# Attention scores in an encoder: stacked high and low parts of queries and keys on 128 partitions, in place of 32-bit products on 64

## The chip, the core and the metric

The kernel runs on one core of a Trainium2 chip. The metric is the device time of one execution in microseconds, median of three runs. TensorE is called PE here, with its weight loads as PEld; VectorE is DVE, ScalarE is ACT, GpSimd is POOL, and SP issues the transfers from HBM.

## The reference, cut to what matters

Two layers, each of them feed-forward, mixer, feed-forward on an input of 256 rows and 1024 columns in float32. The change lies in the mixer's attention.

```python
def hybrid_mixer(x, w_in, sc_conv_w, attn_sink, cc_conv_w, cc_conv_b, cc_ln_g, cc_ln_b, w_out):
    ...
    z = x @ w_in
    sc_b, sc_c, sc_h, q, k, v, cc_a, cc_gate = jnp.split(z, IN_OFFSETS, axis=-1)
    y_sc = sc_b * depthwise_conv(sc_c * sc_h, sc_conv_w)
    q = rope(q.reshape(b, s, N_Q_HEADS, HEAD_DIM), positions)      # 8 heads of 64
    k = rope(k.reshape(b, s, N_KV_HEADS, HEAD_DIM), positions)     # 2 heads of 64
    v = v.reshape(b, s, N_KV_HEADS, HEAD_DIM)
    y_att = banded_window_attention(q, k, v, attn_sink)
    u = cc_a * jax.nn.sigmoid(cc_gate)
    u = depthwise_conv(u, cc_conv_w) + cc_conv_b                   # 31 taps, 256 channels
    y_cc = jax.nn.silu(layer_norm(u, cc_ln_g, cc_ln_b))
    return jnp.concatenate([y_sc, y_att, y_cc], axis=-1) @ w_out

def reference(x, ...):
    for l in range(DEPTH):
        x = layer_norm(ALPHA * x + 0.5 * swiglu(x, ffn1_w_gu[l], ffn1_w_down[l]), ...)
        x = layer_norm(ALPHA * x + hybrid_mixer(x, ...), ...)
        x = layer_norm(ALPHA * x + 0.5 * swiglu(x, ffn2_w_gu[l], ffn2_w_down[l]), ...)
    return x
```

## The kernel before

**Products.** Nearly every float32 product is made as three products of high and low parts (`mm3`: high by high, high by low, low by high), with the parts in the type `F32R`. `split` makes the parts: ACT casts the high part (L96), and DVE subtracts it from the source to get the low part (L97). Weights come in blocks of 128 by 2048 through `fetch` (SP) and `emit_block` (cast and subtract). In each mixer nine of its blocks are listed in `POOL_BLOCKS`; the low part of these is made on POOL in four pieces. A block's buffers come free when its last product has read them, and the cast of a later block waits for that.

**The scores** are the exception: `scores(t, i)` (L542 to L551) takes the turned queries `qT` and keys `kT` in plain float32, 64 partitions (one head's channels) at a time, one product for each head, and adds the window mask by a bf16 product with the identity. A call is a unit of four heads; there are four units in a layer, two for each half of the rows. `q_turned` and `k_turned` transpose on PE into a PSUM bank and copy the bank to SBUF on ACT.

**The mixer** runs in this order: the gate's and queries' projections, keys and values (`kv`), the convolution's three projections (`proj_c` into `psc`, `psh`, `psb`), and in between the four attention units: scores `S_`, softmax, transposes of the probabilities `T_`, product with the values `V_`. The 31 taps of the conformer convolution for two channel groups (62 instructions in a layer, L531 and L533, accumulated in two PSUM banks) run on DVE; `fill(n)` puts n of them into the program at places where DVE was thought to have room, and the rest follows ahead of `T_(3)`. When the last tap is done, PE transposes the convolution's result (`cc_norm`), and the last parts of the output projection (`w_out`, `w_out2`) and the norm at the mixer's boundary follow. `T_(3)`, `w_out2(0, 2)`, `cc_norm`, `V_(3)`, `w_out2(1, 2)`, `cc_out`, `w_out2(1, 0)` and `w_out2(0, 1)` stand in this order in the program.

```python
        w_out2(0, 0)
        fill(62)
        T_(3)
        w_out2(0, 2)
        uns = cc_norm()
        V_(3)
        accs.append([bank() for _ in range(2)])
        new_norm = Norm()
        w_out2(1, 2)
        cc_out(uns)
        w_out2(1, 0)
        w_out2(0, 1)
```

**Order and buffers.** A scheduler places the instructions of each engine in an order of its own, by the program's order and its idea of when each is ready; on the chip each engine runs its list in that order and waits at an instruction whose inputs or buffers are not ready. The pool `mm` has four PSUM banks; while the taps run, two of them hold the convolution, and two are left for everything that is called `tmp`. The pool `gbp` has one buffer, tag `gb`, for the gains and biases of a boundary's norm; it is not in use during the attention.

Of the kernel before, what the change touches and what calls it, by code (L numbers as in the profile page):

```python
# [8 lines left out]
F32 = mybir.dt.float32  # L9
F32R = mybir.dt.float32r  # L10
BF16 = mybir.dt.bfloat16
AF = mybir.ActivationFunctionType
ALU = mybir.AluOpType
# [3 lines left out]
P = 128  # L17
D = 1024
S = 256
# [5 lines left out]
HD = 64  # L25
# [21 lines left out]
def encoder(ctx: ExitStack, tc: tile.TileContext, head_in, xt_in, x_in, w_in, gb_in, small_in, rope_in, out):  # L47
    nc = tc.nc
# [7 lines left out]
    gbp = pool("gbp", 1)  # L56
    st = pool("st", 4)
    mx = pool("mx", 1)
# [29 lines left out]
    def tmp_bank():  # L88
        return phase["pool"].tile([P, 512], F32, tag="mm", name="tmp")
# [113 lines left out]
    def transpose(ps, srcs):  # L203
        for i, a in enumerate(srcs):
            nc.tensor.transpose(ps[:, i * P:(i + 1) * P], a, ident)  # L205
# [252 lines left out]
    def mixer(l, norm):  # L458
# [11 lines left out]
        nc.gpsimd.memset(upad, 0.0)  # L470
        ppad = mx.tile([P, 2, S + 2], F32, tag="ppad", name="ppad")
        nc.gpsimd.memset(ppad, 0.0)
        kT = mx.tile([P, S], F32, tag="kT", name="kT")
        half = HD // 2
        chan = lambda a: a.rearrange("p (c n) -> p c n", c=2)

# [22 lines left out]
        def q_turned(r):  # L499
            pq = tmp_bank()  # L500
            transpose(pq, [r[:, c * P:(c + 1) * P] for c in range(4)])
            q = mx.tile([P, 4, P], F32, tag="qT", bufs=2, name="qT")
            nc.scalar.copy(q.rearrange("p c n -> p (c n)"), pq)
            return q

        def k_turned(t, r):
            pk = tmp_bank()
            transpose(pk, [r[:, 0:P]])
            nc.scalar.copy(kT[:, t * P:(t + 1) * P], pk[:, 0:P])

        def kv(t, w):
            ps = tmp_bank()
# [29 lines left out]
        def scores(t, i):  # L542
            mo = 1 - t
            scs = [chan(bank()) for _ in range(2)]
            for c in range(2):
                for j in range(2):
                    hp = slice(j * HD, (j + 1) * HD)
                    nc.tensor.matmul(scs[j][:, c, :], qT[t][hp, 2 * i + c, :], kT[hp, :], start=True, stop=False)
                for j in range(2):
                    nc.tensor.matmul(scs[j][:, c, mo * P:(mo + 1) * P], ident_b, mask[:, t, :], start=False, stop=True)  # L550
            return scs  # L551
# [81 lines left out]
        qT, vn, rk = [], [], []  # L633
        ga, q = bank(), bank()
# [7 lines left out]
        ga, q = bank(), bank()  # L642
# [12 lines left out]
        v, rk0 = kv(0, wkv)  # L655
        vn.append(v)
        fill(6)
        v, rk1 = kv(1, wkv)
# [3 lines left out]
        fill(6)  # L662
        proj_c(psc, wc, 0)
        qT.append(q_turned(r1))
        k_turned(0, rk0)
        k_turned(1, rk1)
        fill(5)
        proj_c(psc, wc, 1)
        scc = big()
# [6 lines left out]
        def S_(u):  # L676
            return scores(u // 2, u % 2)
# [41 lines left out]
        scs = S_(3)  # L719
# [144 lines left out]
```

## Time and profile before

| what | value |
|---|---|
| median of 3 runs | 935.26 us (935.13 to 937.06) |
| the profiled execution: its time, its span | 937.28 us, 935.5 us |
| PE busy | 921.8 us (99%) |
| DVE busy | 645.4 us (69%) |
| ACT busy | 458.1 us (49%) |
| POOL busy | 116.9 us (12%) |
| mean granted clock of PE | 0.995 |

The profiled execution took 2.0 us more than the median. The shares are averages over the whole span. The mixers, which the change touches, are about 216 to 285 us and 678 to 745 us after the span's start.

### The profile page before, as it was taken

How to read it: one execution, taken by the hardware profiler on the slowest of the kernel's cores; microseconds unless marked ns; L12 is line 12 of the kernel's file. 1: busy time of each engine (PE TensorE's matmuls, PEld its weight loads, DVE VectorE, ACT ScalarE, POOL GpSimd, SP SyncE). 2: the span in 40 equal slices, each digit the busy share in tenths (PEclk: the TensorE clock that was granted, in tenths of full speed). 3: DMA queues.
4: the chain of work that ended last, by engine and by line, in shares of the span. 5: the costliest groups of instructions: out<-in, count | busy, mean ns of one | idle time of the engine just before them, and what ended most of it. 6: DMA issues, size and time to landing. Idle time of an engine off the chain costs nothing.

```text
span 935.5 us, 12113 instructions
## 1 busy us (share of the span) xinstructions
PE 921.8 (99%) x4900; PEld 778.7 (83%) x4900; DVE 645.4 (69%) x811; ACT 458.1 (49%) x593; POOL 116.9 (12%) x108
## 2 busy tenths in 40 slices
PE   9999999999999999999999999999999999999996
PEld 6888888888777888888888888888887788888885
DVE  6966556789967756665777665667799766666545
ACT  6644554345744554445345445454456455444530
POOL 0010000009282000000000000000274800000000
PEclk9999999999999999999999999999999999999998
DMA  9976465546234655454456545544551366555301
GB/s 345 376 249 257 175 222 183 180 140 224 88 102 181 257 211 195 178 187 177 179 187 230 213 180 198 202 171 150 216 190 57 139 247 224 189 180 188 128 1 45
DMA packets 25976, 174.01 MB, mean 186 GB/s; under 512 B 2880, under 2 KB 3136, under 8 KB 5696
## 3 DMA queue, kind: packets, MB, share of 16 engines
q1 hardware_dynamic: 25920, 173.24, 51.5%
q8 instruction: 38, 0.62, 0.3%
q14 instruction: 18, 0.15, 0.0%
HBM read 172.18 MB, written 1.05 MB: 185 GB/s over the span
## 4 chain that ended last, share of the span: by engine, by line
PE 88%; DVE 7%; ACT 1%; POOL 1%; issue 1%; DMA 1%; SPq 0%; DVEq 0%; ACTq 0%
PE wide L170 28%; PE wide L174 15%; PE bank L153 9%; PE bank L154 9%; PE bank L155 9%; PE bank L181 4%; PE bank L185 4%; PE bank L182 4%; DVE tmp L533 3%; PE bank L195 1%; PE tmp L205 1%; POOL lo L97 1%; PE tmp L596 1%; PE bank L205 1%; DVE x L234 1%
## 5 line engine op out<-in xcount | busy, mean ns | idle before, releaser
L97 DVE TENSOR_TENSOR lo<-raw,hi 128x2048 fp32r<-128x2048 f32 (+2 forms) x175 | 317.1, 1825 | 211.1 <-ACT hi L96 210.8
L96 ACT CAST hi<-raw 128x2048 fp32r<-128x2048 f32 (+2 forms) x247 | 306.4, 1270 | 241.2 <-PE wide L170 154.2
L170 PE MATMUL wide<-xT,hi 128*128 128x512 f32 x1152 | 274.1, 390 | 0.0
L170 PEld LDWEIGHTS wide<-xT,hi 128*128 128x128 f32 x1152 | 213.9, 188 | 43.0
L174 PEld LDWEIGHTS wide<-xT,lo 128*128 128x128 f32 x1152 | 147.7, 191 | 5.6
L174 PE MATMUL wide<-xT,lo 128*128 128x256 f32 x1152 | 149.4, 283 | 0.0
L153 PE MATMUL bank<-hi,hh 128*128 128x512 f32 x352 | 137.7, 391 | 0.0
L154 PE MATMUL bank<-lo,hh 128*128 128x512 f32 x352 | 137.4, 390 | 0.0
L155 PE MATMUL bank<-hi,hl 128*128 128x512 f32 x352 | 137.0, 389 | 0.0
L97 POOL TENSOR_TENSOR lo<-raw,hi 128x512 fp32r<-128x512 f32 x72 | 95.9, 1366 | 67.2 <-ACT hi L96 66.8
L228 POOL TENSOR_TENSOR rstd<-ve,mhalf 128x1 f32<-128x1 f32 x12 | 11.5, 961 | 672.0 <-DVE ve L227 672.0
L155 PEld LDWEIGHTS bank<-hi,hl 128*128 128x128 f32 x352 | 66.1, 188 | 14.0
L153 PEld LDWEIGHTS bank<-hi,hh 128*128 128x128 f32 x352 | 66.2, 188 | 12.7
L154 PEld LDWEIGHTS bank<-lo,hh 128*128 128x128 f32 x352 | 66.2, 188 | 12.3
L96 ACT CAST hh<-big 128x512 fp32r<-128x512 f32 x36 | 22.3, 620 | 110.2 <-DVE big L358 110.2
L181 PE MATMUL bank<-hi,xT 128*128 128x512 f32 x160 | 64.7, 404 | 0.0
L182 PE MATMUL bank<-lo,xT 128*128 128x512 f32 x160 | 62.6, 391 | 0.0
L366 DVE TENSOR_TENSOR big<-wide,big 128x512 f32<-128x512 f32 x72 | 49.2, 684 | 6.9 <-ACT big L365 6.9
L533 DVE SCALAR_TENSOR_TENSOR tmp<-upad,wc,tmp 128x256 f32<-128x256 f32 x116 | 49.7, 477 | 0.2
L365 ACT COPY big<-wide 128x512 f32<-128x512 f32 x72 | 42.3, 587 | 11.9 <-PE wide L174 11.6
L185 PE MATMUL bank<-hi,xT 128*128 128x512 f32 x160 | 43.2, 392 | 0.0
L97 DVE TENSOR_TENSOR hl<-big,hh 128x512 fp32r<-128x512 f32 x36 | 24.9, 693 | 24.0 <-ACT hh L96 24.0
(130 smaller groups left out, 890.5 us busy)
## 6 DMA issues: line engine op xcount, KB each, us to landing
raw<-in_w SPq DMA_DIRECT2D x152, 1024.0 KB, 4.8
gb<-in_gb SPq DMA_DIRECT2D x6, 1024.0 KB, 4.9
raw<-in_w SPq DMA_DIRECT2D x4, 512.0 KB, 7.5
head<-in_head SPq DMA_DIRECT2D x4, 384.0 KB, 4.6
raw<-in_w SPq DMA_DIRECT2D x4, 256.0 KB, 7.7
x<-in_x SPq DMA_DIRECT2D x2, 512.0 KB, 5.7
out<-x SPq DMA_DIRECT2D x4, 256.0 KB, 2.1
xraw<-in_xt SPq DMA_DIRECT2D x2, 256.0 KB, 8.0
```

The source lines that it names most:

```text
L96: nc.scalar.copy(hi, src)
L97: (eng or nc.vector).tensor_tensor(lo, src, hi.bitcast(F32), ALU.subtract)
L153: nc.tensor.matmul(ps, ah, bh, start=first, stop=False)
L154: nc.tensor.matmul(ps, ah, bl, start=False, stop=False)
L155: nc.tensor.matmul(ps, al, bh, start=False, stop=last)
L170: nc.tensor.matmul(ps[:, c], w[0][:, k, cs], xT[:, :, k], start=k == 0, stop=False)
L174: nc.tensor.matmul(ps[:, c, 0], w[1][:, k, cs], xT_h[:, k], start=False, stop=k == KC - 1)
L181: nc.tensor.matmul(ps, xT_h[:, kk, t, :], w[0][:, k, :], start=kk == 0, stop=False)
L182: nc.tensor.matmul(ps, xT_h[:, kk, t, :], w[1][:, k, :], start=False, stop=False)
L185: nc.tensor.matmul(ps, xT_l[:, kk, t, :], w[0][:, k, :], start=False, stop=kk == KC - 1)
L366: nc.vector.tensor_tensor(av, ps[:, :, 0], av, ALU.add)
L533: nc.vector.scalar_tensor_tensor(dst, upad[:, c, k:k + S], wc2[:, c, k:k + 1], part, op0=ALU.mult, op1=ALU.add)
```

## The change

Queries and keys are each split into a high and a low part, and the parts of one head are laid on both halves of the 128 partitions. For head j of the two key heads, `qT[:, j]` has the high part on the partitions of the head and the low part on the other 64; `kT[:, j, 0]` has the key's high part on both halves and `kT[:, j, 1]` its low part on both. Two products over 128 partitions then give the sum of all four products of parts. `keep`, in the slot of `gb`, holds the keys and the first half's queries; the second half's queries stay in a tile of their own with one buffer. Both key transposes now go into one PSUM bank, and one call of `k_turned` makes all of `kT`. For a layer this takes away two ACT copies of 128x512 and two of 128x128; it adds four ACT casts of 64x512 and four DVE subtracts of the same size for the queries (two halves of the rows, two heads), and four ACT casts and four DVE subtracts of 64x256 for the keys (two heads, two halves of the partitions).

```diff
-        kT = mx.tile([P, S], F32, tag="kT", name="kT")
+
+        keep = gbp.tile([P, 2, D], F32, tag="gb", name="keep").bitcast(F32R)
+        kT = keep[:, 0].rearrange("p (j x n) -> p j x n", j=2, x=2)
...
             transpose(pq, [r[:, c * P:(c + 1) * P] for c in range(4)])
-            q = mx.tile([P, 4, P], F32, tag="qT", bufs=2, name="qT")
-            nc.scalar.copy(q.rearrange("p c n -> p (c n)"), pq)
+            if qT:
+                q = mx.tile([P, 2, 4, P], F32R, tag="qT", name="qT")
+            else:
+                q = keep[:, 1].rearrange("p (j c n) -> p j c n", j=2, c=4)
+            for j in range(2):
+                own, other = (slice(i * HD, (i + 1) * HD) for i in (j, 1 - j))
+                flat = q[:, j].rearrange("p c n -> p (c n)")
+                nc.scalar.copy(flat[own], pq[own])
+                nc.vector.tensor_tensor(flat[other], pq[own], flat[own].bitcast(F32), ALU.subtract)
             return q
 
-        def k_turned(t, r):
+        def k_turned(rs):
+
             pk = tmp_bank()
-            transpose(pk, [r[:, 0:P]])
-            nc.scalar.copy(kT[:, t * P:(t + 1) * P], pk[:, 0:P])
+            transpose(pk, [r[:, 0:P] for r in rs])
+            for j in range(2):
+                own = slice(j * HD, (j + 1) * HD)
+                for half in range(2):
+                    to = slice(half * HD, (half + 1) * HD)
+                    nc.scalar.copy(kT[to, j, 0], pk[own, 0:S])
+                for half in range(2):
+                    to = slice(half * HD, (half + 1) * HD)
+                    nc.vector.tensor_tensor(kT[to, j, 1], pk[own, 0:S], kT[own, j, 0].bitcast(F32), ALU.subtract)
...
             for c in range(2):
                 for j in range(2):
-                    hp = slice(j * HD, (j + 1) * HD)
-                    nc.tensor.matmul(scs[j][:, c, :], qT[t][hp, 2 * i + c, :], kT[hp, :], start=True, stop=False)
+                    for part in range(2):
+                        nc.tensor.matmul(scs[j][:, c, :], qT[t][:, j, 2 * i + c, :], kT[:, j, part], start=part == 0, stop=False)
...
         qT.append(q_turned(r1))
-        k_turned(0, rk0)
-        k_turned(1, rk1)
+        k_turned((rk0, rk1))
```

The scheduler's order moves too. The first place is PE's list around the key transposes of layer 0. Before, they (`tmp_1936`, `tmp_1939`) stand inside `proj_c(psc)`'s second half (`tmp_1886`), each in a bank of its own:

```order
L205 MATMUL tmp_1936<-ident_85,big_1829 128x128 [waits Activation_49]
L153 MATMUL tmp_1886<-xT_96,hi38_1729 128x256
L154 MATMUL tmp_1886<-xT_96,hi38_1729 128x256
L155 MATMUL tmp_1886<-xT_96,lo38_1730 128x256
L153 MATMUL tmp_1886<-xT_96,hi38_1729 128x256
L205 MATMUL tmp_1939<-ident_85,big_1880 128x128 [waits DVE_49,Activation_49]
```

Now both go into one bank (`tmp_1941`, the one that the second queries' transposes had before), behind the whole of that projection (now `tmp_1888`), and the first scores (`bank_1983`) stand inside the next one (`tmp_2020`, which is `psh`):

```order
L155 MATMUL tmp_1888<-xT_96,lo38_1730 128x256
L205 MATMUL tmp_1941<-ident_85,big_1831 128x128 [waits DVE_49,PE_49]
L205 MATMUL tmp_1941<-ident_85,big_1882 128x128
L153 MATMUL tmp_2020<-xT_96,hi39_1760 128x256 [waits Activation_49]
L154 MATMUL tmp_2020<-xT_96,hi39_1760 128x256
L155 MATMUL tmp_2020<-xT_96,lo39_1761 128x256
L153 MATMUL tmp_2020<-xT_96,hi39_1760 128x256
L154 MATMUL tmp_2020<-xT_96,hi39_1760 128x256
L565 MATMUL bank_1983<-keep_1616 128x256 [waits Activation_49]
```

The first of the key transposes now waits for DVE, where the second queries' last subtract reads that bank.

The second place is DVE's list behind the rotation of the last keys. Before, 15 taps stand there in a row (L533), and the first unit's maximum (L558) follows. Now the subtracts of the second queries (L512) and of the keys (L526) stand between the taps (L550 by the new numbers); these are the rows from the second of the two query subtracts on:

```order
L512 TENSOR_TENSOR qT_1936<-tmp_1931,qT_1936 64x512 [waits Activation_49]
L550 SCALAR_TENSOR_TENSOR tmp_1771<-upad_1612,wc2_1608,tmp_1771 128x256 [waits DVE_49]
L550 SCALAR_TENSOR_TENSOR tmp_1772<-upad_1612,wc2_1608,tmp_1772 128x256 [waits DVE_49]
L550 SCALAR_TENSOR_TENSOR tmp_1771<-upad_1612,wc2_1608,tmp_1771 128x256 [waits DVE_49]
L550 SCALAR_TENSOR_TENSOR tmp_1772<-upad_1612,wc2_1608,tmp_1772 128x256 [waits DVE_49]
L526 TENSOR_TENSOR keep_1616<-tmp_1941,keep_1616 64x256 [waits PE_49,Activation_49]
L526 TENSOR_TENSOR keep_1616<-tmp_1941,keep_1616 64x256
L550 SCALAR_TENSOR_TENSOR tmp_1771<-upad_1612,wc2_1608,tmp_1771 128x256 [waits DVE_49]
L550 SCALAR_TENSOR_TENSOR tmp_1772<-upad_1612,wc2_1608,tmp_1772 128x256 [waits DVE_49]
L575 TENSOR_REDUCE mxs_1998<-bank_1983 128x2 [waits PE_49]
L526 TENSOR_TENSOR keep_1616<-tmp_1941,keep_1616 64x256 [waits Activation_49]
```

The taps that were there move to the end: 16 of them now stand in a row as the last of the layer, where 9 did.

The third place is PE's list at the end of the mixer. Before, the transposes of the convolution's result (`tmp_2385`, `tmp_2386`) follow on the output projection's block `hi41` for the first half of the rows (`bank_2316`), with the products of the last unit's values between them (L596), and `hi41` for the second half (`bank_2418`) comes next:

```order
L155 MATMUL bank_2316<-hi41_1835,yhl_1622 128x512
L205 MATMUL tmp_2385<-ident_85,big_1768 128x128 [waits DVE_49,PE_49]
L205 MATMUL tmp_2386<-ident_85,big_1768 128x128 [waits PE_49]
L596 MATMUL tmp_2411<-big_2364,vn_1827 64x256 [waits Activation_49]
L205 MATMUL tmp_2385<-ident_85,big_1768 128x128 [waits DVE_49]
L205 MATMUL tmp_2386<-ident_85,big_1768 128x128
L596 MATMUL tmp_2411<-big_2364,vn_1878 64x256
L596 MATMUL tmp_2411<-big_2371,vn_1827 64x256 [waits DVE_49]
L596 MATMUL tmp_2411<-big_2371,vn_1878 64x256
L153 MATMUL bank_2418<-hi41_1835,yhh_1621 128x512 [waits PE_49]
```

Now twelve products of the block `hi43` (into `bank_2341` and `bank_2342`, the last of them in the first row here) stand ahead of these transposes (now `tmp_2411`, `tmp_2412`):

```order
L155 MATMUL bank_2342<-hi43_2045,yhl_1620 128x512
L205 MATMUL tmp_2411<-ident_85,big_1770 128x128 [waits DVE_49,PE_49]
L205 MATMUL tmp_2412<-ident_85,big_1770 128x128
L613 MATMUL tmp_2437<-big_2390,vn_1829 64x256 [waits Activation_49]
L205 MATMUL tmp_2411<-ident_85,big_1770 128x128 [waits DVE_49]
L205 MATMUL tmp_2412<-ident_85,big_1770 128x128
L613 MATMUL tmp_2437<-big_2390,vn_1880 64x256
L613 MATMUL tmp_2437<-big_2397,vn_1829 64x256 [waits DVE_49]
L613 MATMUL tmp_2437<-big_2397,vn_1880 64x256
L153 MATMUL bank_2444<-hi41_1837,yhh_1621 128x512 [waits PE_49]
```

Before, those twelve stood behind `hi42`'s products for the second half. So the last read of `hi41` has moved behind them, and with it the cast of the block that takes its buffer (`hi46`, of the feed-forward behind the mixer).

## Rows read from the trace of the kernel before

**Rows 1.** The page, part 1: busy time of each engine.

```profile
PE 921.8 (99%) x4900; PEld 778.7 (83%) x4900; DVE 645.4 (69%) x811; ACT 458.1 (49%) x593; POOL 116.9 (12%) x108
```

**Rows 2.** Chain that ended last, layer 0's mixer: start, us, what.

```profile
222.79 5.88 DVE tmp L533 x15
...
265.99 0.63 ACT hi L96
...
278.25 0.97 POOL rstd L228
279.25 2.45 DVE x L234 x2
...
284.25 1.19 PE bank L185 x4
```

**Rows 3.** Stretches: length, busy of PE, PEld, DVE, ACT, POOL, then granted clock.

```profile
216.00:260.00 44.00, 43.24 (x306) 35.29 (x305) 42.39 (x106) 28.66 (x83) 26.11 (x22) 0.96 0.35 123
678.00:722.00 44.00, 43.24 (x314) 35.13 (x314) 43.27 (x107) 28.94 (x83) 26.53 (x22) 1.00 0.36 128
240.00:244.00 4.00, 4.00 (x24) 3.90 (x23) 3.57 (x8) 4.00 (x14) 3.90 (x4) 0.60 0.00 0
```

**Rows 4.** Timeline of DVE: start, us, engine, line, what [idle before].

```profile
222.72 5.96 DVE L533 SCALAR_TENSOR_TENSOR tmp<-upad,wc,tmp 128x256 f32<-128x256 f32 x15
...
230.18 1.26 DVE L559 SCALAR_TENSOR_TENSOR nm<-mxs,nsink 128x4 f32<-128x4 f32 x1
...
252.64 0.15 DVE L559 SCALAR_TENSOR_TENSOR nm<-mxs,nsink 128x4 f32<-128x4 f32 x1
...
259.08 0.87 DVE L533 SCALAR_TENSOR_TENSOR big<-upad,wc,tmp 128x256 f32<-128x256 f32 x2
...
720.40 0.86 DVE L533 SCALAR_TENSOR_TENSOR big<-upad,wc,tmp 128x256 f32<-128x256 f32 x2
```

**Rows 5.** Timeline of PE at the end of the mixers, columns as in rows 4.

```profile
260.61 0.38 PE L205 MATMUL tmp<-ident,big 128*128 128x128 f32 x2
...
262.88 0.50 PE L153 MATMUL bank<-hi,yhh 128*128 128x512 f32 x1
...
265.74 0.60 PE L205 MATMUL tmp<-ident,big 128*128 128x128 f32 x4
...
721.60 0.38 PE L205 MATMUL tmp<-ident,big 128*128 128x128 f32 x2
```

**Rows 6.** Groups by line and shape, DVE and ACT: busy, mean ns.

```profile
L533 DVE SCALAR_TENSOR_TENSOR tmp<-upad,wc,tmp 128x256 f32<-128x256 f32 x116 | 49.7, 477 | 0.2
...
L97 DVE TENSOR_TENSOR xT<-tmp,xT 128x512 fp32r<-128x512 f32 x20 | 13.6, 682 | 1.3 <-ACT xT L96 1.3
...
L97 DVE TENSOR_TENSOR yhl<-tmp,yhh 128x256 fp32r<-128x256 f32 x8 | 3.4, 421 | 1.9 <-ACT yhh L96 1.7
...
L503 ACT COPY qT<-tmp 128x512 f32<-128x512 f32 x4 | 2.3, 586 | 2.2 <-PE tmp L205 2.2
```

**Rows 7.** Timeline of PE at the first scores and the third unit's.

```profile
225.93 0.28 PE L154 MATMUL tmp<-xT,hi 128*128 128x256 f32 x1
226.05 0.28 PE L155 MATMUL tmp<-xT,lo 128*128 128x256 f32 x1
226.26 0.70 PE L548 MATMUL bank<-kT,qT 64*128 64x256 f32 x4
226.90 0.28 PE L550 MATMUL bank<-mask,ident_b 128*128 128x128 bf16 x2
...
237.59 0.70 PE L548 MATMUL bank<-kT,qT 64*128 64x256 f32 x2 [0.40 <-ACT pr L564]
238.50 0.70 PE L548 MATMUL bank<-kT,qT 64*128 64x256 f32 x2 [0.22 <-ACT pr L564]
```

**Rows 8.** Timeline of POOL in layer 0's mixer.

```profile
211.53 21.11 POOL L97 TENSOR_TENSOR lo<-raw,hi 128x512 fp32r<-128x512 f32 x16 [17.55 <-ACT hi L96]
...
256.24 5.16 POOL L97 TENSOR_TENSOR lo<-raw,hi 128x512 fp32r<-128x512 f32 x4 [3.15 <-ACT hi L96]
```

## The prediction

> **What bounds the kernel now.** The busy times come first: PE is busy for 921.8 of 935.5 us, so nearly every stretch is PE's [rows 1]. What else can move the end must be a place where PE waits, or where another engine's late work makes it wait. The chain of waits through layer 0's mixer shows these places: DVE's taps (15 in a row, 5.88 us), and then at the boundary a chain that leaves PE aside: ACT's cast of `hi46` at 265.99, POOL's low pieces behind it, POOL's `rstd` at 278.25, DVE's L234 at 279.25, and PE's first products of the next feed-forward (L185) at 284.25 [rows 2]. `rstd` stands in POOL's list behind three, then five pieces that hang on the casts of `hi46` and `hi47`. So from the cast to the feed-forward it is 18.3 us of ACT, POOL and DVE, and PE has only the rest of the output projection to put beside it. I call the start of this cast A. Whatever delays A by a microsecond delays the layer by one, as long as POOL's queue stays the last to come.
>
> What sets A is PE: the last read of block `hi41`, just ahead of 265.74 [rows 5]. And PE comes there by two paths. One is its own work. The other is the convolution: the last two taps end at 259.08 + 0.87 = 259.95, PE begins the transposes of the result at 260.61, that is 0.66 us later and without an idle time of its own [rows 4, 5]. In layer 1 the taps end at 721.26 and PE is there at 721.60, a slack of 0.34. So both paths come to the place within a microsecond. The stretches show that DVE has no room ahead of it: from 216 to 260 us it is busy for 42.39 of 44.00 us (1.61 idle), in layer 1 for 43.27 of 44.00 (0.73 idle) [rows 3].
>
> **The change part by part.** *Scores on PE.* Before, the four records of a pair of heads take 226.90 - 226.26 = 0.64 us; a full product of 256 columns in `F32R` starts 0.12 us behind the one ahead (226.05 - 225.93) [rows 7]. Now there are four full ones in their place: 0.48. That saves 0.16 for a pair, 0.32 for a unit, 1.28 for a layer's four units. The masks stay. The bounds are nothing and 1.28, since bf16 masks now stand next to `F32R` products in a mixed order, and no row shows that change of type; I take 1.28.
>
> A rule of the Trainium skill speaks against this term. FP8 and Floating Point Precision, section TensorE Precision Notes, says that a true float32 product goes through the array in four passes. Two half-array heads side by side would then take, as an estimate, 4 x 0.12 = 0.48 us by our pitch, the same as now. The row has 0.64 and not 0.48, so by the row there is something to save; by the rule, nothing.
>
> *PE's stalls.* At the third unit PE waited 0.40 and 0.22 us for the exponentials that free its banks [rows 7], and in the stretch behind this, 240 to 244 us, its granted clock was 0.60, part of it at the lower level: 4 x 0.40 = 1.6 us lost [rows 3]. Layer 1 has the mean clock 1.00 in the whole stretch. The new order puts the first transposes of probabilities inside the products of `psb`, so I take both stalls (0.62) and the clock's loss as gone.
>
> New ones come at the keys. After the last rotation DVE (free at 222.72) has five taps ahead of the second queries' first subtract: 222.72 + 5 x 0.40 = 224.7, with 0.40 a tap from 15 in 5.96 us [rows 4]. The subtract takes 0.60 (below), the next cast on ACT waits for it and takes about what the copy L503 did, 0.59 [rows 6], and the second subtract ends at 225.3 + 0.6 + 0.6 = 226.5. PE is at the key transposes at about 225.8 (it came to the first score at 226.26 with them already done). So it waits some 0.7 there, and then the first scores wait for the keys' casts behind these transposes, and those behind them for DVE's subtracts. Such a cast is at most the 0.586 us of the copy of twice the columns (L503) [rows 6]; I take 0.65 for both waits, 1.35 in all, with bounds of 0 (all covered by products of `psh`) and 2.5 (each of four casts and subtracts late by itself).
>
> *Twelve products moved ahead.* The block `hi43` for the first half of the rows now stands ahead of the convolution's transposes. From 262.88 to 265.74 twelve such products took 2.86 us [rows 5]. They aren't new work, but they are now ahead of A.
>
> So by PE's own path A moves by 2.86 - 1.28 - 0.62 + 1.35 = +2.3 us in layer 1, and by 1.6 less, +0.7, in layer 0.
>
> *DVE's new subtracts.* A layer has four of 64x512 and four of 64x256. The nearest rows are the same operation from PSUM on 128 partitions: 682 and 421 ns [rows 6]. Such records overlap by 0.08 (15 taps at their mean of 477 ns would be 7.2 us, they took 5.96) [rows 4, 6], so one takes about 0.60 and 0.34 of DVE's time: 4 x 0.60 + 4 x 0.34 = 3.8 us. No row has 64 partitions on DVE. If the time went with the partitions, it would be 1.9; I take 3.8, since a record's time follows the columns in all rows (128x512 to 128x256: 682 to 421). The subtracts stand among the taps, and taps that lose their place go to the end: 16 in the last row now. So the last tap moves by 3.8 less what DVE's idle time takes up.
>
> By this path A moves in layer 0 by 3.8 - 0.66 (slack) = 3.1 at most, and by 1.5 if all 1.61 of idle time is used; in layer 1 by 3.5 at most and 2.7 at least. Half of the idle time is behind waits that the new order has too, so I take the middle: +2.3 and +3.1. Both are over PE's path (+0.7, +2.3), so DVE decides.
>
> *ACT.* Its two copies of 128x512 become four casts near the same 0.59 [rows 6], and the keys' two small copies four casts of half that width: at most 4 x 0.59 = 2.4 us more in a layer. ACT is busy for 28.66 of the 44 us [rows 3], so this costs nothing but the waits counted at the keys; without that cover at most 2.4. *The slot of `gb`*: its load is now issued behind the last score, in the order of SP behind the block after the next; the norm that reads it is at 279.25 (L234) [rows 2], behind all attention. Hidden by the last unit's work and the output projection, so I take nothing; if it were late, L233 just ahead of `rstd` would wait.
>
> **The sum**, against the profiled execution: 937.28 + 2.3 + 3.1 = 942.7. This execution is 2.0 above the median, about the 1.6 that the clock took in layer 0. An execution without that would have both layers like layer 1: 935.26 + 2 x 3.1 = 941.5. I predict **942.0**.
>
> **The rivals.** *Slower still, by the waits of small DVE operations.* While POOL makes low pieces (211.53 to 232.64), `nm` took 1.26 us on DVE, and 0.15 at 252.64 with POOL idle [rows 4, 8]. With the taps later, one or two of the last unit's small operations fall on POOL's next pieces from 256.24 on, 1.1 us each: 942.0 + 2 x 1.1 to 2 x 2.2 = 944 to 946.5. A further slow stretch of the clock behind the new stalls would add 1.6. Chance 0.2.
>
> *The same.* DVE's subtracts cost half (1.9 us, the time going with the partitions), and PE's new stalls are hidden. Then DVE's path is -0.4 to +1.2 in layer 0 and +0.8 to +1.6 in layer 1, and PE's 2.86 - 1.28 - 0.62 = +1.0 in layer 1. The sum is 937.3 plus 0.6 to 2.8, and 2.0 less against the median: 935.9 to 938.1. For it speaks only that no row shows the price. Chance for something within 0.2% (1.9 us, about what a measurement of this kernel can tell from no change): 0.14.
>
> *Faster.* The place is the boundary: PE has 2 x (1.28 + 0.62) = 3.8 us less to do, 5.4 with the clock. If POOL's queue is not what holds the feed-forward, because ACT can cast `hi46` from a buffer that comes free earlier, then A does not count and the end is 937.28 - 5.4 = 931.9. It decides from the point where the taps end by 260.6 and the last read of `hi41` is no later than 265.74. For it: PE is 99% busy. Against: the chain goes through POOL from about 266.7 to 279.2, and the twelve products stand ahead of that read. Chance 0.2.
>
> *The scores save nothing.* PE's path becomes +2.0 and +3.6; DVE's still decides in layer 0, and the sum is 937.28 + 2.3 + 3.6 = 943.2. Against it: a pair takes 0.64 and not 0.48 before. Chance 0.05. This is the time by the Trainium skill's rule named above.
>
> **How the numbers follow.** The forecast has 0.41, with its own range of 939.5 to 944.5: 1.5 + 2.7 and 3.1 + 3.5 against the execution's time (941.5 to 943.9), and about 2 less against the median. Slower by over 0.2% is forecast, its own further rival and the scores without a saving: 0.41 + 0.2 + 0.05 = 0.66. The range of 932.5 to 947 takes in the same, most of the second and the near half of the faster cases; less than 2 in 10 lie outside.
>
> **What would show it.** In the changed kernel's rows: L565 at 0.12 from start to start; a gap on PE ahead of the key transposes that DVE ends; L512 near 0.60 and L526 near 0.34 apart; the last taps ending 2 to 4 us later than before, measured from the first kernel's same place (the last queries' product), and the convolution's transposes following at once; the cast of `hi46` later by as much; from it to L185 again 18.3 us. I am wrong if subtracts on 64 partitions take half, if the taps end early, or if `hi46` comes no later.

## The result: slower by 1.3%, about twice what was forecast

The changed kernel took 948.11 us (median of 4 runs, 946.49 to 948.73), the kernel before 935.19 in the same measurement. The ratio on record is 1.0127, with a 95% interval of 1.0101 to 1.0153; the two medians alone give 1.0138. The forecast was 942.0, with a range up to 947.0. The profiled execution took 947.96 us, 10.68 more than the profiled execution before.

The page of the changed kernel, its parts 1 and 2: busy time of the engines, and PE's granted clock in 40 slices.

```profile
PE 925.0 (98%) x4900; PEld 784.5 (83%) x4900; DVE 653.4 (69%) x827; ACT 463.2 (49%) x601; POOL 117.6 (12%) x108
...
PEclk9999999999998999999999999999999899999998
```

The clock's row of the kernel before:

```profile
PEclk9999999999999999999999999999999999999998
```

DVE has 8.0 us more work than in [rows 1], two layers of about 4. PE's busy time rose too, although it has less to do: busy time includes what it does at a slower clock. Three slices have an 8 now. The last had it before too; the other two are the two boundaries behind the mixers.

To compare places, take a mark ahead of the change: the mixer's first transposes on PE, at 204.46 and 666.90 us before and at 203.77 and 671.31 now. These are layer 1's rows of the two kernels (timeline; start, us, engine, line, what, and in brackets the idle time before it and who ended it). First the kernel before:

```profile
666.90 0.38 PE L205 MATMUL tmp<-ident,big 128*128 128x128 f32 x2
...
726.97 2.18 ACT L96 CAST hi<-raw 128x512 fp32r<-128x512 f32 x4 [2.62 <-PE bank L155]
...
738.60 1.01 POOL L228 TENSOR_TENSOR rstd<-ve,mhalf 128x1 f32<-128x1 f32 x1
740.58 0.66 PE L205 MATMUL tmp<-ident,x 128*128 128x128 f32 x4 [0.28 <-DVE x L234]
742.28 0.66 PE L205 MATMUL tmp<-ident,x 128*128 128x128 f32 x4 [0.35 <-DVE x L234]
...
744.80 1.21 PE L185 MATMUL bank<-hi,xT 128*128 128x512 f32 x4
```

And the changed one:

```profile
671.31 0.38 PE L205 MATMUL tmp<-ident,big 128*128 128x128 f32 x2
...
729.27 0.86 DVE L550 SCALAR_TENSOR_TENSOR big<-upad,wc,tmp 128x256 f32<-128x256 f32 x2
...
735.32 2.18 ACT L96 CAST hi<-raw 128x512 fp32r<-128x512 f32 x4 [2.66 <-PE bank L155]
...
746.93 1.00 POOL L228 TENSOR_TENSOR rstd<-ve,mhalf 128x1 f32<-128x1 f32 x1
749.92 1.12 PE L205 MATMUL tmp<-ident,x 128*128 128x128 f32 x4 [2.60 <-DVE x L234]
751.59 1.12 PE L205 MATMUL tmp<-ident,x 128*128 128x128 f32 x4 [0.56 <-DVE x L234]
...
755.92 1.36 PE L185 MATMUL bank<-hi,xT 128*128 128x512 f32 x4
```

Take 4.41 (671.31 - 666.90) off the second column of times, and each place shows its delay. The last tap: 730.13 against 721.26 [rows 4], +4.46. The cast of `hi46`: +3.94. `rstd`: +3.92. The second transposes of the first rows: +4.90. The feed-forward's L185: +6.71. Up to `rstd` the delay is what DVE's taps passed on. Behind it come two more pieces: 1.0 us between `rstd` and the transposes, and 1.8 between the transposes and L185. Layer 0 reads the same. Its rows of the kernel before that [rows 2, 4] don't have:

```profile
204.46 0.38 PE L205 MATMUL tmp<-ident,big 128*128 128x128 f32 x2
...
280.05 0.66 PE L205 MATMUL tmp<-ident,x 128*128 128x128 f32 x4 [0.74 <-DVE x L234]
281.74 0.66 PE L205 MATMUL tmp<-ident,x 128*128 128x128 f32 x4 [0.33 <-DVE x L234]
```

And of the changed one (`rstd`, the transposes and L185 stand further down):

```profile
203.77 0.38 PE L205 MATMUL tmp<-ident,big 128*128 128x128 f32 x2
...
261.72 0.86 DVE L550 SCALAR_TENSOR_TENSOR big<-upad,wc,tmp 128x256 f32<-128x256 f32 x2
...
267.77 2.19 ACT L96 CAST hi<-raw 128x512 fp32r<-128x512 f32 x4 [2.66 <-PE bank L155]
```

With the mark 0.69 earlier, the taps are at +3.32, the cast +2.47, `rstd` +2.02, the second transposes +3.19, L185 +5.00. The two layers make 11.7; the mixer of layer 0 began 0.69 earlier, and a net 0.3 came back elsewhere.

The first extra piece is on DVE and POOL. These are the timelines of both in layer 0:

```profile
278.58 2.24 DVE L233 SCALAR_TENSOR_TENSOR x<-x,mv,gb 128x512 f32<-128x512 f32 x2
280.75 3.43 DVE L234 SCALAR_TENSOR_TENSOR x<-x,rstd,gb 128x512 f32<-128x512 f32 x2
```

```profile
279.58 1.00 POOL L228 TENSOR_TENSOR rstd<-ve,mhalf 128x1 f32<-128x1 f32 x1
280.55 6.46 POOL L97 TENSOR_TENSOR lo<-raw,hi 128x512 fp32r<-128x512 f32 x4
```

L234 for the two halves takes 3.43 us, where [rows 2] had 2.45. POOL's first piece of `hi48` now starts the moment `rstd` ends (280.55), 0.20 ahead of L234, and L234 has to wait for it. Before, L234 came first, at 279.25, and POOL's piece 0.16 behind it (in layer 1 0.62 behind):

```profile
279.41 5.94 POOL L97 TENSOR_TENSOR lo<-raw,hi 128x512 fp32r<-128x512 f32 x4 [0.20 <-ACT hi L96]
```

The second extra piece is PE's clock. Behind 2.81 us without work PE runs slowly; the timeline of PE in layer 0:

```profile
282.56 1.12 PE L205 MATMUL tmp<-ident,x 128*128 128x128 f32 x4 [2.81 <-DVE x L234]
284.24 1.12 PE L205 MATMUL tmp<-ident,x 128*128 128x128 f32 x4 [0.56 <-DVE x L234]
285.00 0.78 PE L181 MATMUL bank<-hi,xT 128*128 128x512 f32 x1
285.58 0.63 PE L182 MATMUL bank<-lo,xT 128*128 128x512 f32 x1
286.00 0.63 PE L181 MATMUL bank<-hi,xT 128*128 128x512 f32 x1
...
288.56 1.24 PE L185 MATMUL bank<-hi,xT 128*128 128x512 f32 x4
```

Products of 512 columns start 0.43 us apart, nearly twice the usual 0.23. The granted clock is 0.50 from 282.1 to 288.8, the lower of its two levels, and 1.00 from 289 on; in layer 1 it is 0.50 from 749.7 to 756.4. The stretches around both boundaries (length, busy of PE, PEld, DVE, ACT, POOL, then the clock):

```profile
282.00:290.00 8.00, 6.88 (x22) 5.48 (x23) 8.00 (x13) 2.21 (x4) 6.01 (x4) 0.57 0.41 162
747.00:756.00 9.00, 5.84 (x19) 4.36 (x18) 9.00 (x13) 4.47 (x9) 7.54 (x6) 0.65 0.41 127
```

Before, PE was idle for 0.74 and 0.33 us at the same place in layer 0, 0.28 and 0.35 in layer 1, and stayed at 1.00. The scheduler had left three products between the two groups of transposes there. In the new order they stand ahead of both, so the idle time is in one piece.

### The profile page after: what moved, and what is told of

Its sections match the earlier page's. It is cut to its first block, busy times and chain, and to the rows that moved or that the text cites. A ratio compares the mean times of both kernels' runs of the same rounds, so it can differ in the third digit from the quotient of the medians.

```text
span 946.2 us, 12149 instructions
## 1 busy us (share of the span) xinstructions
PE 925.0 (98%) x4900; PEld 784.5 (83%) x4900; DVE 653.4 (69%) x827; ACT 463.2 (49%) x601; POOL 117.6 (12%) x108
## 4 chain that ended last, share of the span: by engine, by line
PE 92%; DVE 5%; ACT 1%; issue 1%; DMA 0%; DVEq 0%; ACTq 0%
PE wide L170 28%; PE wide L174 15%; PE bank L153 9%; PE bank L155 9%; PE bank L154 9%; PE bank L181 4%; PE bank L182 4%; PE bank L185 4%; PE tmp L153 2%; PE tmp L154 2%; DVE tmp L550 2%; PE tmp L155 2%; PE tmp L205 2%; PE bank L195 1%; PE bank L205 1%; PE bank L565 1%
## 5 line engine op out<-in xcount | busy, mean ns | idle before, releaser
L181 PE MATMUL bank<-hi,xT 128*128 128x512 f32 x160 | 66.7, 417 | 0.0
L550 DVE SCALAR_TENSOR_TENSOR tmp<-upad,wc,tmp 128x256 f32<-128x256 f32 x116 | 49.9, 479 | 0.2
L185 PE MATMUL bank<-hi,xT 128*128 128x512 f32 x160 | 43.4, 393 | 0.0
```

Source lines behind the costliest of these rows:

```text
L181: nc.tensor.matmul(ps, xT_h[:, kk, t, :], w[0][:, k, :], start=kk == 0, stop=False)
L185: nc.tensor.matmul(ps, xT_l[:, kk, t, :], w[0][:, k, :], start=False, stop=kk == KC - 1)
L550: nc.vector.scalar_tensor_tensor(dst, upad[:, c, k:k + S], wc2[:, c, k:k + 1], part, op0=ALU.mult, op1=ALU.add)
```

## The experiments

The kernel before, measured again beside each group of runs, took 935.16 to 935.99 us (medians), so a difference between medians of different groups is good to about 0.8 us. "From the mark" is meant as above.

**First: which part of the change delays, and does the clock matter?** Copies on ACT in place of DVE's subtracts. They put the high parts where the low parts were, so this kernel leaves out the low parts:

```diff
-                nc.vector.tensor_tensor(flat[other], pq[own], flat[own].bitcast(F32), ALU.subtract)
+                nc.scalar.copy(flat[other], pq[own])
...
-                    nc.vector.tensor_tensor(kT[to, j, 1], pk[own, 0:S], kT[own, j, 0].bitcast(F32), ALU.subtract)
+                    nc.scalar.copy(kT[to, j, 1], pk[own, 0:S])
```

> The changed kernel with its eight DVE subtracts of a layer replaced by ACT copies of the same source and size into the same places (the low parts are left out: the places hold the high parts again). Theory A, that DVE's subtracts push the taps to the end of the mixer, and that this delays the boundary: the last tap ends about 3.8 us earlier than in the changed kernel, the cast of hi46 comes 2 to 4 us earlier a layer, the idle time of PE at the boundary falls from 2.8 to under 1.5 us and its clock stays at 1.00 there: 936 to 940. Rival B, that only the new order of PE's list (twelve products ahead of the convolution's transposes) delays the boundary: the last tap ends earlier but the cast of hi46 doesn't, and the time stays at 946 to 949.

945.79 us, ratio 1.0116 (1.0100 to 1.0131). Neither theory's range has this number, and the run doesn't tell them apart: in layer 1 the taps end 1.4 us earlier than in the changed kernel (both from the mark), the cast of `hi46` 0.7. The copies delay ACT's casts of weights, POOL's pieces with them, and DVE's small operations then meet those pieces (`nm`, `es` and `den` take 2.3 us more than before in that mixer). The work was moved, not removed.

The kernel before, with subtracts of the same sizes that nobody reads, and one bank for the keys:

```diff
+            for j in range(2):
+                own, other = (slice(i * HD, (i + 1) * HD) for i in (j, 1 - j))
+                nc.vector.tensor_tensor(junk[other, 1, 0:512], pq[own], flat[own], ALU.subtract)
...
+                    nc.vector.tensor_tensor(junk[to, 0, j * S:(j + 1) * S], pk[own, 0:S], kT[own], ALU.subtract)
```

> The kernel before with eight DVE subtracts of the same sizes a layer, whose results nobody reads, and the keys' transposes in one bank; the scores stay 32-bit products on 64 partitions. Theory A: DVE's load alone brings the delay; the boundary is as late as in the changed kernel and PE has 1.3 us more to do a layer to cover it: 943 to 949. Rival B (the scores' products or the order that they bring are the cause): 935 to 938.

949.44 us, ratio 1.0150 (1.0134 to 1.0165). So the new scores aren't needed to get the loss: the subtracts that prepare them are enough. The taps end 4.8 us later than before in layer 1, as in the changed kernel (4.5).

The last read of `hi41` moved ahead of the convolution's norm:

```diff
+        accs.append([bank() for _ in range(2)])
+        w_out2(1, 2)
         uns = cc_norm()
         V_(3)
-        accs.append([bank() for _ in range(2)])
         new_norm = Norm()
-        w_out2(1, 2)
```

> The changed kernel with the output projection's block hi41 for the second half of the rows written ahead of the convolution's norm, so that its last read needn't wait behind the last unit's values; everything is computed. Theory A, that the time of the cast of hi46 sets the boundary: the cast is 1.5 to 2 us earlier a layer, and the time falls by 3 to 8 us (the larger if the clock's slow stretch goes too): 940 to 945. Rival B, that the statistics of the norm are the later of the two: no change, 947 to 949.

952.99 us, ratio 1.0191 (1.0176 to 1.0207): slower, which neither theory had. The cast of `hi46` came 2.3 us earlier, as written, and brought its pieces on POOL forward. POOL's timeline in layer 0:

```profile
266.13 2.52 POOL L97 TENSOR_TENSOR lo<-raw,hi 128x512 fp32r<-128x512 f32 x2 [2.76 <-ACT hi L96]
268.61 1.08 POOL L628 TENSOR_TENSOR rstd<-ve,mhalf 128x1 f32<-128x1 f32 x2
...
284.18 0.99 POOL L228 TENSOR_TENSOR rstd<-ve,mhalf 128x1 f32<-128x1 f32 x1
```

Two of them now stand ahead of the convolution norm's `rstd` (L628), which starts at 268.61 and not at 265.72; everything behind that norm is late, and the boundary's `rstd` comes at 284.18 instead of 279.58. So the time of that cast alone doesn't set the boundary: what stands where in POOL's list does as well.

Products that nobody reads, in PE's idle time at the boundary:

```diff
+            pd = tmp_bank()
+            flat = mask.rearrange("p t n -> p (t n)")
+            nc.tensor.matmul(pd[:, 0:2], ident, norm.mv[0], start=True, stop=True)
+            for i in range(warm):
+                nc.tensor.matmul(pd[:, 0:S], ident_b, flat, start=True, stop=True)
         norm.turn(0, 0)
```

> The changed kernel with 24 bf16 products of 256 columns into a bank that nobody reads, placed on PE between the end of the output projection and the transposes of the first rows, where PE is idle for 2.8 us in the changed kernel. Theory C, that PE's idle time there brings the stretch of half clock behind it and that this is some 2.4 us of a layer: granted clock 1.00 in the stretch behind the boundary, 942 to 945. Rival D, that the clock falls for another reason, or that the stretch costs nothing because something else is late: 947 to 950.

943.18 us, ratio 1.0084 (1.0067 to 1.0101), as theory C had it: 4.9 us less than the changed kernel by adding work. The idle time ahead of the first transposes is 0.69 and 0.55 us, and the same stretches have the full clock:

```profile
282.00:290.00 8.00, 7.41 (x36) 5.98 (x37) 7.83 (x14) 3.36 (x6) 5.30 (x4) 1.00 0.48 186
745.00:754.00 9.00, 8.12 (x48) 6.44 (x46) 8.83 (x13) 3.94 (x8) 7.33 (x6) 1.00 0.48 169
```

The taps, the cast and L234's 3.43 us are unchanged in this run, and the transposes come within 0.1 us of where they were (from the mark). Three products of the output projection stand between the two groups of transposes again, as in the kernel before, but they fill time in which PE would wait for L234's second half. So the clock is worth 4.9 us by itself.

**Second: DVE's load.** No subtracts, and zeros written once by POOL instead:

```diff
-                nc.vector.tensor_tensor(flat[other], pq[own], flat[own].bitcast(F32), ALU.subtract)
...
-                    nc.vector.tensor_tensor(kT[to, j, 1], pk[own, 0:S], kT[own, j, 0].bitcast(F32), ALU.subtract)
...
+        nc.gpsimd.memset(keep[:, 0].bitcast(F32), 0.0)
```

> The changed kernel without the subtracts and without anything in their place: the places of the low parts are set to zero once by POOL at the start of each mixer, where POOL is idle (the low parts are left out). ACT's casts and PE's products stay. Theory A (DVE's subtracts delay the taps, these the boundary): the last tap comes 3 to 4 us earlier a layer than in the changed kernel, the cast of hi46 within 1 us of the kernel before, and PE's clock stays at 1.00 at the boundary: 933 to 938. Rival B (the twelve products of hi43 ahead of the convolution's transposes delay the boundary by themselves): hi46 2 us late a layer although the taps are early: 941 to 947.

942.28 us, ratio 1.0068 (1.0053 to 1.0083). The mechanism is theory A's, the sum is not: the time is in rival B's range. From the mark, the taps end 2.9 us (layer 0) and 3.0 us (layer 1) earlier than in the changed kernel, and the cast of `hi46` 2.1 and 2.2: that is DVE's share. But L234 is still hindered and PE still idle for 2.85 us in one piece, with the slow clock behind it:

```profile
279.07 3.43 DVE L234 SCALAR_TENSOR_TENSOR x<-x,rstd,gb 128x512 f32<-128x512 f32 x2 [0.44 <-POOL rstd L228]
```

So about half of the loss needs no subtract at all. In layer 1 this run's cast of `hi46` is 1.7 us later than before, but only 0.3 of it is rival B's: PE comes to the convolution's transposes 0.6 us after the taps' end, where it was 0.34. The other 1.4 us are the taps', which end that much later than before without any subtract; `nm`, `es` and `den` take 1.8 us more there, as in the run with ACT's copies.

The keys' parts for both heads and halves at once, and then also the probabilities' second copies on ACT:

```diff
-            transpose(pk, [r[:, 0:P] for r in rs])
+            transpose(pk, [r[:, (1 + j) * P:(2 + j) * P] for j in range(2) for r in rs])
+            pk = pk.rearrange("p (j n) -> p j n", j=2)
+            nc.scalar.copy(kT[:, :, 0], pk)
+            nc.vector.tensor_tensor(kT[:, :, 1], pk, kT[:, :, 0].bitcast(F32), ALU.subtract)
...
-                if j == 0:
-                    nc.scalar.copy(pT, pp)
-                else:
-                    nc.vector.tensor_copy(pT, pp)
+                nc.scalar.copy(pT, pp)
```

> The changed kernel with the keys' parts made for both heads and both halves at once: the rotation writes each head twice side by side, four transposes (two more) fill a whole bank, one ACT cast and one DVE subtract of 128x512 take the place of four and four of 64x256; everything is computed. DVE's work falls by 4 x 0.34 - 0.60 - 0.28 = 0.5 us a layer, ACT's by about 0.6. Theory A: 0.5 us earlier a layer, 945 to 948; the clock's slow stretch stays. Rival E, that the chain of casts and subtracts before the first scores counts more than DVE's load: 940 to 944.

948.89 us, ratio 1.0143 (1.0116 to 1.0170): no gain, and 0.9 us over theory A's range. The 0.5 us of DVE didn't reach the taps: from the mark they end 1.2 us later than in the changed kernel in layer 0, and at the same time in layer 1. Why is not shown.

> As the run with the keys' parts made at once, and the second copy of the turned probabilities of each unit on ACT in place of DVE (four copies of 128x512 a layer, 0.60 us each); everything is computed. DVE's work is then 3.8 - 0.5 - 2.4 = 0.9 us a layer over the kernel before. Theory A: the taps end about 1 us later than before, the boundary with them, and PE's saving covers part of it: 934 to 940, without the slow stretch. Rival F, that ACT's work then delays the probabilities and the casts of weights by as much: 943 to 949.

941.45 us, ratio 1.0066 (1.0046 to 1.0085), between the two ranges, 1.5 us above theory A's. The taps end within 0.6 us of the kernel before in both layers, the cast of `hi46` comes 1.1 us late in layer 1 (the products of `hi43` ahead of it), and yet 6 us are lost: L234 takes 3.43 us and PE waits for 2.81 and 2.64 in one piece.

The same relief in the kernel before:

> The kernel before with the second copy of the turned probabilities on ACT in place of DVE; everything is computed. It takes 2.4 us a layer off DVE and puts it on ACT. Theory A, with PE's own path only 0.3 to 0.7 us behind DVE's in the kernel before: the taps end 2 us earlier, the boundary at most 0.5 us a layer: 933.5 to 935.5. Rival F, ACT is late instead: 936 to 941.

934.91 us, ratio 0.9991 (0.9972 to 1.0010), no change that the median can tell. But its ten executions reach from 932.57 to 939.21 us, and in the profiled one, the fastest, the taps end 3.1 us earlier than before in both layers and L185 starts 2.2 and 1.9 us earlier: there the relief reached the boundary by more than the 0.5 us expected.

**Third: POOL's queue at the boundary.** The block `hi48` on DVE:

```diff
-ON_POOL = range(7, 16)
+ON_POOL = range(7, 15)
```

> The changed kernel with the block hi48's low part on DVE in place of POOL; everything is computed. In the changed kernel POOL's first piece of hi48 starts as rstd ends, and the second half of DVE's L234 waits for it (3.43 us for the two instead of 2.44). In the new order of DVE's list the pieces of hi48 stand behind L234. Theory G, that this collision costs 1 us a layer and adds to PE's idle time: L234 takes 2 x 0.75 us, the transposes of the first rows come 1.5 to 2 us earlier, PE's idle time falls to 1 to 2 us and the slow stretch of its clock with it: 939 to 944. Rival H, that the start of the feed-forward is held by something else (lo48 is late in its turn): 946 to 950.

941.50 us, ratio 1.0065 (1.0050 to 1.0080), as theory G had it: 6.6 us less than the changed kernel, with `rstd` where it was. L234 now takes 1.40 us, and all eight transposes follow on each other. (Before the change it took 2.45 [rows 2], so this run takes away 2.0 us a layer there, where the change had added 1.0; the kernel before gets the same relief in the last run below.)

```profile
280.95 1.40 DVE L234 SCALAR_TENSOR_TENSOR x<-x,rstd,gb 128x512 f32<-128x512 f32 x2
```

```profile
281.74 1.32 PE L205 MATMUL tmp<-ident,x 128*128 128x128 f32 x8 [1.79 <-DVE x L234]
```

This agrees with the Trainium skill, SBUF — State Buffer, section SBUF: two separate sides: a DVE operation with two inputs from SBUF and a GpSimd operation that reads SBUF exclude each other, and the one that starts first holds the ports until it is done. L234 reads `x` and `gb` from SBUF; with a POOL piece it is 3.43 us, without 1.40. After an idle time of 1.79 us in layer 0 the clock was still 0.83 over the ten microseconds from 280; after 1.64 us in layer 1 it was 1.00 over those from 745. So the 6.6 us are the collision with a part of the clock's loss, and not the collision alone.

With `hi47` on DVE as well (`range(7, 14)`):

> The changed kernel with hi47's and hi48's low parts on DVE in place of POOL; everything is computed. Then only the four pieces of hi46 stand ahead of rstd on POOL. Theory A's last part, that the cast of hi46 reaches the feed-forward through POOL's queue alone: rstd comes when the statistics do, about 1 us earlier than in the changed kernel (the statistics are ready at 278.7 there, rstd starts at 279.6), and L234 isn't hindered: 939 to 944. Rival I, that DVE's eight pieces delay the sums of the first rows (L221) instead: 946 to 950.

950.60 us, ratio 1.0164 (1.0148 to 1.0179): rival I. DVE's timeline shows where:

```profile
272.96 3.38 DVE L97 TENSOR_TENSOR lo<-raw,hi 128x2048 fp32r<-128x2048 f32 x1 [1.35 <-ACT hi L96]
276.27 0.68 DVE L97 TENSOR_TENSOR yhl<-big,yhh 128x512 fp32r<-128x512 f32 x1
```

The whole block's subtract of 3.38 us stands ahead of the last low part of the output projection's input (`yhl`), which took 1.01 us from 272.27 on in the changed kernel. It is now done 3.7 us later, and the sums of the first rows with it. The same on the run with DVE's relief:

> The run with the keys' parts made at once and the probabilities' copies on ACT, with hi47's and hi48's low parts on DVE; everything is computed. From its 941.45: rstd ahead by up to 1 us a layer, L234 free of POOL (1 us), PE's idle time and the slow clock gone (1.7 us a layer): 934 to 938, and below the kernel before if PE's saving of 2.6 us comes through: 932 to 935. Rival I (the statistics get late): 940 to 944.

946.91 us, ratio 1.0121 (1.0104 to 1.0138), rival I again, past its upper number.

> The kernel before with the probabilities' second copies on ACT and hi47's and hi48's low parts on DVE; everything is computed, scores as 32-bit products. If POOL's queue sets the boundary there too, rstd comes up to 3 us earlier and the output projection becomes the bound: 930 to 934. If not (the convolution's norm or the projection are as late): 934 to 937.

940.61 us, ratio 1.0058 (1.0039 to 1.0077): outside both, for the same subtract.

**Fourth: together.** The last four runs combine what had helped alone; their code is that of the runs above. The first still leaves out the low parts.

> The changed kernel without the subtracts (low parts left out, zeros in their place) and with hi48's low part on DVE. If DVE's subtracts, the collision and the clock are all of the 12.9 us: as the kernel before or less, 932 to 936. If the order of PE's list and the key transposes behind the projection cost something by themselves: 937 to 941.

936.70 us, ratio 1.0007 (0.9996 to 1.0017): between its two ranges, and within 0.2% of the kernel before. The subtracts and the collision, with the clock that hangs on them, are 11.4 of the 12.9 us.

> The run with the keys' parts made at once and the probabilities' copies on ACT (941.45), with the block hi48's low part on DVE; everything is computed. If the collision at L234 and the clock behind it are what is left of that run's 6 us: 1 us a layer for L234, 1 us a layer from the transposes that follow, up to 1.7 us a layer for the clock: 934 to 938. If hi46's cast alone (1.1 us a layer late there) and the 12 products ahead of the convolution's transposes count: 938 to 941.

935.13 us, ratio 0.9993 (0.9983 to 1.0004). This computes everything, and all of the loss is gone.

> As the run with all three reliefs of DVE and POOL, with ten bf16 products of 256 columns, which nobody reads, on PE ahead of the transposes of the first rows. If a slow stretch of the clock is left in that run: 2 to 4 us faster than it, 932 to 935. If none is left: as fast or 0.5 us slower, since the ten products can delay what stands behind them.

935.01 us, ratio 0.9985 (0.9974 to 0.9996): by the ratio 1.4 us faster than the kernel before, with an interval that ends just short of 1 (by the medians, 935.01 and 935.99, it is 1.0 us). The clock is 1.00 behind the boundaries. Against the run without the ten products the medians differ by 0.1 us.

> The kernel before with the probabilities' second copies on ACT and hi48's low part on DVE; everything is computed. There L234 takes 2.44 us, 1 us more than alone: 932 to 935 if the transposes of the first rows come earlier by that; 935 to 938 if lo48 is then late or the end is set elsewhere.

934.76 us, ratio 0.9981 (0.9969 to 0.9992). By the median, the 32-bit scores with the same relief are as fast as the best version with the new scores. By single executions they are ahead: four of the twelve took 932.8 to 933.1 us, with a mean granted clock of 0.997, and none of the 24 with the new scores took less than 934.16. The other eight had 0.993 to 0.996; in the profiled one the clock falls in layer 1's mixer (0.62 over 698.0 to 702.5). So what the new scores save on PE doesn't reach the end, even when all that they cost is hidden.

## Why the prediction was right in its way and wrong in its size

**Scores on PE: right.** The forms of the changed kernel (busy, mean ns), and one unit of its timeline:

```profile
L565 PE MATMUL bank<-keep 128*128 128x256 f32 x32 | 6.7, 316 | 0.1
```

```profile
239.20 0.43 PE L565 MATMUL bank<-keep,qT 128*128 128x256 f32 x2
239.47 0.23 PE L567 MATMUL bank<-mask,ident_b 128*128 128x128 bf16 x1
239.51 0.48 PE L565 MATMUL bank<-keep,qT 128*128 128x256 f32 x2
239.82 0.23 PE L567 MATMUL bank<-mask,ident_b 128*128 128x128 bf16 x1
239.86 0.36 PE L155 MATMUL tmp<-xT,lo 128*128 128x256 f32 x1
```

A pair with its two masks takes 0.66 us (239.20 to 239.86), where [rows 7] have 0.64 and then the masks, 0.85 from 226.26 to the next pair:

```profile
227.11 0.70 PE L548 MATMUL bank<-kT,qT 64*128 64x256 f32 x4
```

That saves 0.19 and not 0.16. The Trainium skill, FP8 and Floating Point Precision, section TensorE Precision Notes, gives a true float32 product four passes. The estimate that was worked out from it, 0.48 us for a pair and nothing to save, doesn't agree with the 0.64 of the trace.

**PE's stalls: the old ones gone as forecast, the new ones of about the size, by another cause.** The third unit starts without a wait (above), and the clock is 1.00 from 216 to 260 us. At the keys PE loses about 1.0 us instead of 1.35, most of it in front of `psh`, for ACT's copy of `psc`:

```profile
225.15 0.41 PE L205 MATMUL tmp<-ident,big 128*128 128x128 f32 x2
226.26 0.38 PE L153 MATMUL tmp<-xT,hi 128*128 128x256 f32 x1 [0.71 <-ACT big L686]
```

**DVE's subtracts: right in price, too low in effect.** The forms:

```profile
L526 DVE TENSOR_TENSOR keep<-tmp,keep 64x256 fp32r<-64x256 f32 x8 | 3.4, 422 | 0.5 <-ACT keep L523 0.4
...
L512 DVE TENSOR_TENSOR qT<-tmp,qT 64x512 fp32r<-64x512 f32 x4 | 2.8, 689 | 0.2
```

64 partitions take what 128 do (682 and 421 ns in [rows 6]). Taken away alone they give back 2.9 and 3.0 us of the taps' end, against 3.8 put in. But the taps end 4.46 us later in layer 1, where the sum had 3.8 less what DVE's idle time takes up. It took nothing up: from the mark to the last tap DVE was idle for 4.65 us (busy for 54.17 of 58.82), and for 3.46 before (50.94 of 54.40). What made it idle longer is not worked out here.

**The twelve products: right.** PE waited 0.24 us for the taps in layer 0, although it had done them (0.26 in layer 1); DVE's path was the later one. They are the later one only where DVE is relieved.

```profile
262.33 0.41 PE L205 MATMUL tmp<-ident,big 128*128 128x128 f32 x2 [0.24 <-DVE big L550]
```

**The cast of `hi46`: right in layer 0, low in layer 1.** Forecast +2.3 and +3.1 us, measured +2.47 and +3.94; the forecast had 3.5 as the most in layer 1.

**From the cast to the feed-forward: this step failed.** "Whatever delays A by a microsecond delays the layer by one, as long as POOL's queue stays the last to come." I took the 18.3 us from the cast to L185 as fixed. They became 20.8 in layer 0 (288.56 - 267.77) and 20.6 in layer 1 (755.92 - 735.32, where 17.8 had been), for two reasons. A piece of POOL now came 0.2 us ahead of DVE's L234, which had come first: 1.0 us a layer, and 6.6 us for the kernel with all that hangs on it. And "PE has only the rest of the output projection to put beside it" was written down as a fact about cover, with no price for its end. The projection's last product started 1.0 us earlier in layer 0 (from the mark; at 279.37 now and at 281.01 before), and the transposes came 3.2 us later. So PE stood idle for 2.6 to 2.8 us in one piece and had the lower clock for nearly 7 us from there on (4.9 us of time for both layers, by the run with the 24 products). A slow stretch of the clock stood among the rivals, at the keys and with 1.6 us; it came at the boundary. With the clock put right, the run was at 943.2, near the forecast's 942.0, but in part by luck: L185 came 7.6 us late there in the two layers, not 5.4, and the rest of the kernel gave 1.8 us back.

The rival of DVE's small operations with a slow stretch added (up to 946.5 + 1.6) has nearly the measured time, but it isn't what happened: `nm`, `es` and `den` take 4.6 us in layer 1 now and took 4.8 before.

The single effects add up to more than the loss (5.8 for the subtracts, 6.6 for the collision, 4.9 for the clock, 12.9 in all), because the collision is part of the idle time, and the idle time is what the clock's stretch follows on. What stays open is why the clock behaved otherwise after idle times as long: in layer 0 of the run with ACT's copies (e1) it stayed at 1.00 after 2.63 us, and in that of the kernel before with subtracts (e2) it fell some 2 us after the end of 2.78 us, with the transposes still at full speed.

Open in part is also why the saving on PE doesn't show in the best version. The scores themselves do save: in layer 1 of the run with all three reliefs (e13) they and their masks take 5.1 us, counted from each start to the next, and 7.0 with the 32-bit scores and the copies on ACT (e8). But PE's busy time from the mark to L185 is not lower, 75.5 us against 74.9, both at a granted clock of 1.00. So other products and transposes take the saving up; why they do is not shown.

## What to carry to other kernels

Work that is added to an engine with no room is paid at the next place where others wait for that engine. Follow the delay from there to the engine that has run out of work, and give the idle time a price of its own: here, idle time of 2.6 to 2.8 us in one piece cost nearly as much again in clock, though not in every run. Where two engines exclude each other, look up which of them starts first and by how much: a margin of 0.2 us is not one to build a sum on. And before a cheaper product is paid for with preparation, ask whether the stage ends on PE at all; here the same relief of DVE and POOL was worth at least as much without the new scores.

## What had not been expected of the hardware

A subtract of 64x512 took 690 ns on DVE and one of 128x512 took 682: half the partitions, the same time. A filler of 24 bf16 products that nobody reads (2.78 us) made the changed kernel 4.9 us faster, through PE's clock: the transposes behind it came when they had come without it.
